# Attention heads three steps later, the first norm's chain in front, and filler transposes on TensorE in a hybrid decoder layer

## The chip, the cores and the metric

One NeuronCore of a Trainium2 chip runs the whole layer. The metric is device time in microseconds (us), the median of several executions. A profiled execution gives the trace that is read below. Engine names are those of the profile: PE is TensorE (PEld its weight loads), DVE is VectorE, ACT is ScalarE, POOL is GpSimd, SP is SyncE, whose queue issues nearly all DMAs.

## The reference

One decoder layer on 256 tokens of width 1024, in float32. A conditioning vector gives shifts, scales and gates by one matrix product. The normed and modulated input goes through one projection whose columns are attention q, k, v (8 heads of 64) and mLSTM q, k (with a causal convolution), v, output gate and gate inputs (4 heads of 128). With 256 tokens the attention is one causal block.

```python
mod = jax.nn.silu(c) @ w_ada[l] + b_ada[l]
sh1, sc1, g1, sh2, sc2, g2 = jnp.split(mod, 6, axis=-1)
h = modulate(x, norm1_g[l], sh1, sc1)          # rms_norm(x) * (1 + sc1) + sh1
proj = h @ w_in[l]
q_a, k_a, v_a, qk_m, v_m, o_m, gates = jnp.split(proj, offs, axis=-1)
attn = merge_heads(moba_attention(rope(q_a), rope(k_a), v_a))
attn = head_rms_norm(attn, attn_out_g[l], ATT_HEADS)
qk_m = jax.nn.silu(causal_conv(qk_m, conv_w[l], conv_b[l]))
hm = mlstm_chunkwise(q_m, k_m * MLSTM_HEAD_DIM ** -0.5, v_m, i_pre, f_pre)
hm = head_rms_norm(hm, mlstm_out_g[l], MLSTM_HEADS) * jax.nn.sigmoid(o_m)
x = x + g1 * (jnp.concatenate([attn, hm], axis=-1) @ w_out[l])
h2 = modulate(x, norm2_g[l], sh2, sc2)
x = x + g2 * hier_moe(h2, ...)                 # 32 experts, top 2 of 8 in the top group
return rms_norm(x, norm_f_g)
```

## The kernel before

All weights stream from HBM through a ring of 23 SBUF slots of 1 MB. A list (`order`) fixes the sequence of the transfers: `wa` (conditioning), `wi` (input projection), `wo` (output projection), then `we`, 192 MB of expert weights. SP issues them in that sequence, each as soon as the slot that it takes has been given back. Everything up to the router, about the first third of the time, is called the front here; after it the experts run quad by quad (`ffn1`, `ffn2`).

Projections keep float32 accuracy by a split of each weight row block: ACT copies it rounded (`whb`, line 210), POOL subtracts (`wlb`, line 211), and PE multiplies three times (lines 494, 495, 497). Four split buffers turn round; `split_to` and `ahead` say how far the splits run ahead of their use.

The start. `xt` (the input) arrives; 16 transposes (`tp`) turn it; four copies take it out of PSUM into `xT`, two on DVE and two on ACT (`x_evac`). Meanwhile ACT squares `xt`, and `norm1_scale` (five small DVE operations, lines 340 to 344) makes the reciprocal norm `r1`; `norm1_rows` spreads it along rows (`rd` on ACT, `rp` on PE, `R1` on ACT). `ada_half(j, h)` computes 256 columns of the conditioning (16 matmuls `adap`, line 404, and a DVE copy into `rowb`), `ada_half_cols` turns them into columns (line 414) and adds the bias (`modc`, line 416). `mod_scale` multiplies `xT` by scale and norm on DVE (line 462), `mod_shift` makes `hh` and the shifted `xT` on ACT (lines 466, 467), `mod_lo` the low part `hl` (line 470). The first projection matmuls `pk` need `hh`, `whb` and `wlb`. Rope angles (two Sin activations on ACT, lines 280 and 284) come right behind. Up to the sixth weight block of k, q and v, the instructions are pinned: their order on the engine is the order of the code.

Behind that, a list scheduler sets the order on each engine, with the order of the code as priority. `pc` are the matmuls of the convolved mLSTM q and k, `po` those of the output gate, `pvm` those of mLSTM v, `op` those of the output projection; each runs over eight k blocks. `side` is a list of attention steps, and `step()` takes one: `attn_s(h)` (scores `s_ps`, DVE row maxima, ACT exponentials `ex`), `attn_t(h)` (transposes `pt_ps`, copied to `ptT`) and `attn_pv(h)` (`pv_ps`). With head 7, `attn_fin` norms all heads on DVE (lines 681 to 689) into `cat`, whose transposes are `ct`. `ml_e(h)` makes the decay matrices (`mb_ps` on PE, `ee` on ACT, a select on POOL), `em_cols` the column `em` (`pmc`, DVE line 711, ACT line 712), `ml_s` and `ml_pv` the mLSTM products (`ms_ps`, `mpv`). `late_rows` computes three more blocks of the conditioning (16 matmuls `adap`, line 431, copied by ACT line 435), `late_cols` their columns (`modp`).

Of the kernel before, what the change touches and what calls it, by code (L numbers as in the profile page):

```python
# [28 lines left out]
MLS = (0, 1, 2, 3)  # L29
CT = (3, 5)  # L30
PIN = 24
MACS = (1, 1, 0, 0)
SLOTS = 23
KEEP = 9
# [3 lines left out]
def tile_hybrid_layer(  # L38
# [11 lines left out]
    nc = tc.nc  # L50
    V, A, G, T = nc.vector, nc.scalar, nc.gpsimd, nc.tensor
# [8 lines left out]
    def pacc(name):  # L60
        return ps.tile([128, 512], F32, name=name, tag="acc", bufs=4)
# [4 lines left out]
    def pA(name):  # L66
        return ps.tile([128, 512], F32, name=name, tag="A", bufs=1)
# [47 lines left out]
    nissued = [0]  # L115
# [3 lines left out]
    def behind(i):  # L119
        ins = i.ins  # L120
        prev = next((x for x in reversed(nc.cur_bb.bb.instructions)
                     if x is not ins and x.engine == ins.engine and x.name not in floating), None)
        tc.add_manual_dep(ins, prev.name, mybir.DependencyInfo(mybir.DependencyClass.NoSync,
                                                               mybir.DependencyReason.DATA), reason="order")

# [2 lines left out]
    def P(i):  # L128
        if pinned[0]:
            behind(i)  # L130
# [2 lines left out]
    keep = [KEEP]  # L133

    def issue():
        kind, j, h = order[nissued[0]][:3]
        part = order[nissued[0]][3:]
        if part == (1,):
            nissued[0] += 1
            behind(nc.sync.dma_start(chunks[kind, j, h][:, 1024:2048], srcs[kind][j, :, h * 2048 + 1024:(h + 1) * 2048]))  # L140
            return
        t = ringp.tile([128, 2048], F32, name=f"w{kind}{j}_{h}", tag="w", bufs=SLOTS)
        chunks[kind, j, h] = t
        nissued[0] += 1
        live[0] += 1
        if part == (0,):
            behind(nc.sync.dma_start(t[:, 0:1024], srcs[kind][j, :, h * 2048:h * 2048 + 1024]))
        elif nissued[0] <= len(order) - 4:
            i = nc.sync.dma_start(t, srcs[kind][j, :, h * 2048:(h + 1) * 2048])
            if nissued[0] < PIN:  # L150
                behind(i)
        elif nissued[0] == len(order):
            for c, n in LAST:
                for key in order[-4:]:
                    src = srcs["e"][key[1], :, h * 2048:(h + 1) * 2048].rearrange("p (f n) -> p f n", f=4)
                    behind(nc.sync.dma_start(chunks[key][:, 4 * c:4 * (c + n)].rearrange("p (f n) -> p f n", f=4),  # L156
                                             src[:, :, c:c + n]))
# [5 lines left out]
    def free(n=1, hold=1):  # L163
        live[0] -= n
        keep[0] += hold
        fill()

    def fill():
        while nissued[0] < len(order) and (live[0] + keep[0] < SLOTS or order[nissued[0]][3:] == (1,)):
            issue()  # L170
# [6 lines left out]

    nc.sync.dma_start(xt, x.rearrange("(t p) d -> p t d", p=128))
    rowb = big("rowb", [128, 2048])
    nc.scalar.dma_start(rowb[:, 1536:1996], colp[:, 96:556])  # L180
    convw = rowb[:, 1536:1568].rearrange("p (i c) -> p i c", i=4)
    wgate = rowb[:, 1568:1632].rearrange("p (k n) -> p k n", k=8)
    wr = rowb[:, 1632:1920].rearrange("p (k n) -> p k n", k=8)
# [10 lines left out]
    def wt(kind, j, k):  # L194
        n = 1024 if kind == "e" else 512
        per = 2048 // n
        return chunks[kind, j, k // per][:, (k % per) * n:(k % per + 1) * n]
# [6 lines left out]
    def split_to(n):  # L204
        while nsplit[0] < min(n, len(subs)):
            i = nsplit[0]
            kind, j, k = subs[i]
            hi, lo = whb[:, i % 4], wlb[:, i % 4]
            src = wt(kind, j, k)
            P(A.activation(hi, src, AF.Copy))  # L210
            G.tensor_tensor(lo, src, hi.bitcast(F32), OP.subtract)  # L211
            parts[kind, j, k] = (hi, lo)
            if k % 4 == 3:
                done()
            nsplit[0] += 1
# [9 lines left out]
    def ahead():  # L225
        split_to(nused[0] + 3)
# [6 lines left out]
    ident = small("ident", [128, 128])  # L233
# [80 lines left out]
    hh = big("hh", [128, 8, S], F32R)  # L314
    hl = big("hl", [128, 8, S], F32R)
    pinned[0] = True
    xps = [pacc(f"tp{kk}") for kk in range(4)]
    for kk in range(4):
        transpose2(xt, kk, xps[kk])

    def x_evac(eng, kk):
        dst, src = xT[:, 2 * kk:2 * kk + 2], xps[kk].rearrange("p (j n) -> p j n", j=2)
        P(V.tensor_copy(dst, src) if eng is V else A.activation(dst, src, AF.Copy))
# [15 lines left out]
    def norm1_scale():  # L339
        P(V.tensor_scalar(v1, ss1, 1.0 / D, EPS, op0=OP.mult, op1=OP.add))  # L340
        P(V.reciprocal(r1, q1))
        P(V.tensor_tensor(q1, r1, r1, OP.mult))
        P(V.scalar_tensor_tensor(q1, q1, -0.5, v1, op0=OP.mult, op1=OP.mult))
        P(V.scalar_tensor_tensor(r1, q1, 1.5, r1, op0=OP.add, op1=OP.mult))
# [66 lines left out]
    def ada_half_cols(half):  # L411
        j, h, p, r = half
        for b in range(2):
            P(T.matmul(p[:, 256 + b:257 + b], r[:, b * 128:(b + 1) * 128], gsel[:, 0:1], start=True, stop=True))
        c0 = 4 * j + 2 * h
        P(V.tensor_tensor(modc[:, c0:c0 + 2], p[:, 256:258], bada[:, c0:c0 + 2], OP.add))
# [6 lines left out]
    def late_cols():  # L423
        j, r = late.pop(0)
        ada_cols(j, r, psm, gsel)
# [34 lines left out]
    def mod_scale(m):  # L460
        for k in range(2 * m, 2 * m + 2):
            P(V.scalar_tensor_tensor(xT[:, k], xT[:, k], a1[:, k:k + 1], R1, op0=OP.mult, op1=OP.mult))

    def mod_shift(m):
        for k in range(2 * m, 2 * m + 2):
            P(A.activation(hh[:, k], xT[:, k], AF.Identity, bias=modc[:, k:k + 1]))
            P(A.activation(xT[:, k], xT[:, k], AF.Identity, bias=modc[:, k:k + 1]))
# [3 lines left out]

    G.memset(wg32, 0.0)
    x_evac(V, 0)
    x_evac(V, 1)
    x_evac(A, 2)
    x_evac(A, 3)
    half = ada_half(2, 0)
    norm1_scale()
    norm1_rows()
    ada_half_cols(half)  # L480
    mod_a1(0)
    half = ada_half(0, 0)
    ahead()
    mod_scale(0)
    ada_half_cols(half)
    mod_shift(0)


    def ip(p, j, k):
        wh, wl = take("i", j, k)  # L490
        ahead()
        ts = [(t, slice(t * 128, (t + 1) * 128)) for t in range(2)]
        for t, tt in ts:
            P(T.matmul(p[t], hh[:, k, tt], wh, start=k == 0, stop=False))  # L494
            P(T.matmul(p[t], hh[:, k, tt], wl, start=False, stop=False))  # L495
        for t, tt in ts:
            P(T.matmul(p[t], hl[:, k, tt], wh, start=False, stop=k == 7))  # L497
# [135 lines left out]
    def attn_s(h):  # L633
        p = psm("s_ps")
        b, o = h // 2, 64 * (h % 2)
        for t in range(2):
            T.matmul(p[:, t * 128:t * 128 + 128 * (t + 1)], qT[o:o + 64, b, t * 128:(t + 1) * 128],  # L637
                     kT[o:o + 64, b, 0:128 * (t + 1)], start=True, stop=True)
        dg = p.rearrange("p (b n) -> p b n", b=4)[:, 0:3:2, :]
        V.tensor_tensor(dg, dg, cmask[:, None, :].to_broadcast([128, 2, 128]), OP.add)  # L640
        V.tensor_reduce(mx[:, h, 0:1], p[:, 0:128], AX.X, OP.max)
        V.tensor_reduce(mx[:, h, 1:2], p[:, 128:384], AX.X, OP.max)
        V.tensor_scalar(mx[:, h], mx[:, h], -0.125, None, op0=OP.mult)
        e = u2("ex", [128, 384])
        for t in range(2):
            A.activation(e[:, t * 128:t * 128 + 128 * (t + 1)], p[:, t * 128:t * 128 + 128 * (t + 1)], AF.Exp,
                         scale=0.125, bias=mx[:, h, t:t + 1], accum_out=rs[:, h, t:t + 1])
        att[h] = e
# [58 lines left out]
    def em_cols():  # L707
        pmc = pY("pmc")
        for t in range(2):
            T.transpose(pmc[:, t * 4:t * 4 + 4], mr[:, t * 128:(t + 1) * 128], ident[0:4, 0:4])  # L710
        behind(V.tensor_tensor(em, nF, pmc[:, 0:8].rearrange("p (t n) -> p t n", t=2), OP.subtract))
        A.activation(em, em, AF.Exp)
# [20 lines left out]


    g1b = wk.tile([128, D], F32, name="g1b", tag="g1b")
    side = [lambda: attn_s(0), lambda: attn_s(1)]

    def t_then_s(h):
        attn_t(h)
# [14 lines left out]
    def step():  # L754
        if side:
            side.pop(0)()
# [3 lines left out]
    for k in range(8):  # L760
        cvk(pc, 3, k)
        step()
        mac(MACS[0])
    conv(pc, 3)
# [4 lines left out]
    for k in range(8):  # L769
        cvk(pc, 4, k)  # L770
        step()
        mac(MACS[1])
    conv(pc, 4)
    while side:
        step()
    free()
    cols()
    row_bcast(modc[:, 20:24], g1b[:, 512:1024])
    A.activation(cv[:, 0:4], cv[:, 0:4], AF.Silu)
    A.activation(cv[:, 4:8], cv[:, 4:8], AF.Silu)  # L780

    po = [pacc("po0"), pacc("po1")]
    em_cols()
    for k in range(8):
        ip(po, 6, k)
        if k % 2 == 0:
            ml_e(k // 2)
        if k in (1, 4, 7):
            late_rows(7 + k // 3)
        if k in (2, 5):  # L790
            late_cols()
    free()
    for t in range(2):
        A.activation(cat[:, t, 512:1024], po[t], AF.Tanh, scale=0.5)
# [574 lines left out]
```

## Time and profile before

| what | value |
|---|---|
| runs shown | 649.70, 648.49, 649.06 us, median 649.06 |
| profiled execution, its own time | 649.01 us |
| its span in the trace | 647.4 us |
| PE busy | 563.3 us, 87% of the span |
| DVE, ACT, POOL busy | 170.2, 144.0, 103.7 us |
| bytes moved by DMA | 248.31 MB, mean 384 GB/s |
| mean granted TensorE clock | 0.973 of full speed |

The span runs from the first to the last instruction; the own time holds 1.61 us more, which lie around it. Busy time of PE is modelled and says that PE had work, not that it ran at its peak. The share of a whole span is a mean over stages with different limits, so the stages are read one by one below.

### The profile page before, as it was taken

To read this page: it belongs to the slowest core of one execution; us is meant where nothing else is said; L and a number is where in the kernel's file an instruction comes from. 1 tells how busy PE (TensorE), PEld (TensorE's weight loads), DVE (VectorE), ACT (ScalarE), POOL (GpSimd) and SP (SyncE) were. 2 spreads that over 40 slices of the span, in tenths; PEclk is the share of its full clock that TensorE was granted. 3 is DMA by queue.
4 is the path that set the end of the run, shared out by engine and by line. 5 is a ranking of instruction groups with operands and counts; after the bars stand their busy time and mean duration, and the time that the engine had idled before them with its cause. 6 is when DMAs were issued, how large, how long until landed. Compare 5 with 4: busy or idle time off the path is not lost.

```text
span 647.4 us, 7994 instructions
## 1 busy us (share of the span) xinstructions
PE 563.3 (87%) x3178; PEld 275.3 (43%) x3178; DVE 170.2 (26%) x448; ACT 144.0 (22%) x306; POOL 103.7 (16%) x98
## 2 busy tenths in 40 slices
PE   4899989999997999998889869877988798889874
PEld 3576878875685444352123214211421332233122
DVE  1533979852745030220002002000100110100013
ACT  5453567854443110000000000000000000001013
POOL 2566746672630000000000000000000000000000
PEclk9799999998996999999989999998999999999998
DMA  8999963699696899999999999999999999999994
GB/s 339 423 425 425 415 264 103 245 353 377 220 403 251 330 427 427 427 425 425 428 428 427 425 427 427 429 426 426 426 428 427 426 425 428 425 426 426 428 383 148
DMA packets 41640, 248.31 MB, mean 384 GB/s; under 512 B 4352, under 2 KB 10624, under 8 KB 12928
## 3 DMA queue, kind: packets, MB, share of 16 engines
q1 hardware_dynamic: 41024, 247.00, 92.5%
q10 hardware_dynamic: 576, 0.76, 0.3%
q8 instruction: 26, 0.43, 0.2%
q14 instruction: 14, 0.11, 0.1%
HBM read 246.70 MB, written 1.05 MB: 383 GB/s over the span
## 4 chain that ended last, share of the span: by engine, by line
DMA 50%; PE 36%; DVE 8%; ACT 2%; SPq 2%; issue 1%; DVEq 0%; ACTq 0%
DMA we<-in_wexp_dram 49%; PE f L1124 4%; PE f1a L1103 3%; PE f1b L1103 3%; PE xg_ps L1024 2%; SPq L156 2%; PE adap L404 1%; PE acc L1136 1%; DVE rowb L366 1%; PE xg_ps L1038 1%; DMA xt<-in_x_dram 1%; DVE ropd L563 1%; PE s_ps L637 1%; PE pk L494 1%; PE pk L495 1%
## 5 line engine op out<-in xcount | busy, mean ns | idle before, releaser
L1103 PE MATMUL f1a<-we,xgt 128*32 128x512 f32 x512 | 134.1, 605 | 30.2 <-DMA we<-in_wexp_dram 30.2
L1103 PE MATMUL f1b<-we,xgt 128*32 128x512 f32 x512 | 133.0, 594 | 0.0
L1124 PE MATMUL f<-we,htb 128*32 128x512 f32 (+2 forms) x576 | 82.8, 572 | 17.3 <-DMA we<-in_wexp_dram 17.3
L211 POOL TENSOR_TENSOR wlb<-wi,whb 128x512 fp32r<-128x512 f32 x56 | 74.6, 1349 | 56.4 <-ACT whb L210 48.8
L1103 PEld LDWEIGHTS f1a<-we,xgt 128*32 128x32 f32 x512 | 23.9, 109 | 105.0 <-DMA we<-in_wexp_dram 81.0
L1103 PEld LDWEIGHTS f1b<-we,xgt 128*32 128x32 f32 x512 | 32.7, 109 | 72.6 <-issue 69.8
L1109 ACT ACTIVATE sab<-f1a 128x256 f32<-128x256 f32 x8 | 3.1, 384 | 247.0 <-PE f1a L1103 247.0
L1110 DVE TENSOR_TENSOR acb<-sab,f1a 128x256 f32<-128x256 f32 x8 | 3.4, 422 | 202.6 <-ACT sab L1109 202.6
L1124 PEld LDWEIGHTS f<-we,htb 128*32 128x32 f32 x576 | 21.2, 113 | 64.9 <-DMA we<-in_wexp_dram 31.6
L210 ACT ACTIVATE whb<-wi 128x512 fp32r<-128x512 f32 x56 | 34.5, 632 | 26.8 <-PE pv L497 7.6
L1130 DVE TENSOR_TENSOR ysb<-f,g2b 128x512 f32<-128x512 f32 (+2 forms) x18 | 11.4, 632 | 93.1 <-PE f L1124 93.1
L1024 PEld LDWEIGHTS xg_ps<-gsb,xt 128*128 128x128 f32 x224 | 26.7, 191 | 13.3 <-issue 7.9
L1029 ACT ACTIVATE xgt<-xg_ps,modc,a 128x128 f32<-128x128 f32 x28 | 10.5, 457 | 93.2 <-PE xg_ps L1024 93.2
L1024 PE MATMUL xg_ps<-gsb,xt 128*128 128x128 f32 x224 | 28.6, 279 | 1.9 <-ACT xgt L1029 1.9
L1136 PE MATMUL acc<-ysb,pwb 128*128 128x512 f32 x56 | 27.3, 613 | 2.5 <-DVE ysb L1130 2.3
L211 POOL TENSOR_TENSOR wlb<-wo,whb 128x512 fp32r<-128x512 f32 x16 | 21.0, 1317 | 23.7 <-ACT whb L210 23.2
L366 DVE SCALAR_TENSOR_TENSOR rowb<-wa,cs,rowb 128x512 f32<-128x512 f32 x21 | 23.9, 1139 | 0.3
L506 PE MATMUL pc<-hl,whb 128*128 128x256 f32 x64 | 18.4, 289 | 0.0
L505 PE MATMUL pc<-hh,whb 128*128 128x256 f32 x64 | 18.2, 286 | 0.0
L1136 PEld LDWEIGHTS acc<-ysb,pwb 128*128 128x128 f32 x56 | 9.6, 189 | 19.2 <-issue 8.9
L507 PE MATMUL pc<-hh,wlb 128*128 128x256 f32 x64 | 17.7, 289 | 0.0
L1012 DVE TENSOR_TENSOR gsb<-iot,posm 128x128 f32<-128x128 f32 x16 | 4.4, 289 | 35.7 <-PE xg_ps L1024 32.1
(371 smaller groups left out, 691.5 us busy)
## 6 DMA issues: line engine op xcount, KB each, us to landing
we<-in_wexp_dram SPq DMA_DIRECT2D x188, 1024.0 KB, 19.6
wa<-in_wada_dram SPq DMA_DIRECT2D x24, 1024.0 KB, 13.6
wi<-in_win_dram SPq DMA_DIRECT2D x8, 1024.0 KB, 18.4
wi<-in_win_dram SPq DMA_DIRECT2D x12, 512.0 KB, 14.0
wo<-in_wout_dram SPq DMA_DIRECT2D x4, 1024.0 KB, 7.2
we<-in_wexp_dram SPq DMA_DIRECT2D x4, 512.0 KB, 16.8
we<-in_wexp_dram SPq DMA_DIRECT2D x8, 256.0 KB, 6.3
xt<-in_x_dram SPq DMA_DIRECT2D x1, 1024.0 KB, 5.7
```

The lines of the kernel that those rows point to most:

```text
L156: behind(nc.sync.dma_start(chunks[key][:, 4 * c:4 * (c + n)].rearrange("p (f n) -> p f n", f=4), src[:, :, c:c + n]))
L210: P(A.activation(hi, src, AF.Copy))
L211: G.tensor_tensor(lo, src, hi.bitcast(F32), OP.subtract)
L366: i = V.scalar_tensor_tensor(r, w, cs[:, k:k + 1], r, op0=OP.mult, op1=OP.add)
L505: T.matmul(o, wh[:, cc], hh[:, k], start=k == 0 and c % 2 == 0, stop=False)
L506: T.matmul(o, wh[:, cc], hl[:, k], start=False, stop=False)
L507: T.matmul(o, wl[:, cc], hh[:, k], start=False, stop=k == 7 and c % 2 == 1)
L1024: T.matmul(p[:, (k % 4) * 128:(k % 4 + 1) * 128], xn[:, t, k * 128:(k + 1) * 128], gsb[:, q % 2, t], start=t == 0, stop=t == 1)
L1103: T.matmul(hid[h][CAP * i:CAP * (i + 1), :], xgb[q % 2][:, k, i * CAP:(i + 1) * CAP], w[:, h * 512:(h + 1) * 512], start=k == 0, stop=k == 7)
L1124: m = T.matmul(py[CAP * i:CAP * (i + 1), 0:n], htb[:, f // 2, o:o + CAP], chunks["e", 3 * (4 * q + i) + 2, dh][:, w0:w0 + n], start=f == 0 ...
L1130: V.tensor_tensor(ysb[q % 2][:, c0:c0 + n], py[:, 0:n], g2b[:, c0:c0 + n], OP.mult)
L1136: T.matmul(acc[b], pwb[:, q % 2, t * 128:(t + 1) * 128], ysb[q % 2][:, h * 512:(h + 1) * 512], start=q == 0, stop=q == NQ - 1 - h)
```

## The change

It has three parts. First, the side list begins with three empty steps, and the steps left over are taken in the output gate's loop (`po`) and behind it, not behind the second convolution; `em_cols` moves behind them. Second, in the start `norm1_scale` stands right behind the first copy, the two copies on ACT stand behind `mod_shift(0)`, only two weight blocks are split ahead and not three, and the transfer of the small tables (`rowb`, 230 KB) leaves ACT's queue and stands sixth among SP's weight transfers. Third, TensorE transposes the identity into an unused PSUM tile: 28 times before `xt` arrives, and 4, 4 and 8 times in the first chain; nothing reads the result.

```diff
+SHIFT = 3
+WARM = 28
...
     def issue():
+        if nissued[0] == 5:
+            behind(nc.sync.dma_start(rowb[:, 1536:1996], colp[:, 96:556]))
         kind, j, h = order[nissued[0]][:3]
...
     rowb = big("rowb", [128, 2048])
-    nc.scalar.dma_start(rowb[:, 1536:1996], colp[:, 96:556])
...
     pinned[0] = True
+    wp = pA("warm")
+
+    def fillers(n):
+        for _ in range(n):
+            P(T.transpose(wp[:, 0:128], ident, ident))
+
+    fillers(WARM)
     xps = [pacc(f"tp{kk}") for kk in range(4)]
...
     x_evac(V, 0)
+    norm1_scale()
     x_evac(V, 1)
-    x_evac(A, 2)
-    x_evac(A, 3)
     half = ada_half(2, 0)
-    norm1_scale()
+    fillers(4)
     norm1_rows()
     ada_half_cols(half)
     mod_a1(0)
     half = ada_half(0, 0)
-    ahead()
+    fillers(4)
     mod_scale(0)
+    split_to(2)
     ada_half_cols(half)
+    fillers(8)
     mod_shift(0)
+    x_evac(A, 2)
+    x_evac(A, 3)
...
-    side = [lambda: attn_s(0), lambda: attn_s(1)]
+    side = [lambda: None] * SHIFT + [lambda: attn_s(0), lambda: attn_s(1)]
...
     conv(pc, 4)
-    while side:
-        step()
-    free()
+    step()
     cols()
...
     po = [pacc("po0"), pacc("po1")]
-    em_cols()
     for k in range(8):
         ip(po, 6, k)
+        step()
         if k % 2 == 0:
             ml_e(k // 2)
...
+    while side:
+        step()
+    free()
+    em_cols()
     free()
```

On ACT at the start, the order before is this, from the squares of `xt` to the first Sin (`hl` is only where the squares are thrown):

```order
L330 ACTIVATE hl,ss_169<-xt 128x1024 x2
L337 ACTIVATE q_177<-ss_169,epsb 128x2
L323 ACTIVATE xT<-tp_151 128x512
L323 ACTIVATE xT<-tp_152 128x512
L349 ACTIVATE rd<-ident,r_176 128x128 x2
L351 ACTIVATE R_179<-rp 128x256
L210 ACTIVATE whb<-wi_0_82 128x512 x2
L210 ACTIVATE whb<-wi_0_84 128x512
L466 ACTIVATE hh<-xT,modc 128x256
```

And of the change, up to the third weight split:

```order
L349 ACTIVATE q_206<-ss_198,epsb 128x2
L361 ACTIVATE rd<-ident,r_205 128x128 x2
L363 ACTIVATE R_208<-rp 128x256
L215 ACTIVATE whb<-wi_0_81 128x512 x2
L478 ACTIVATE hh<-xT,modc 128x256
L479 ACTIVATE xT<-xT,modc 128x256
L335 ACTIVATE xT<-tp_180 128x512
L335 ACTIVATE xT<-tp_181 128x512
L285 ACT_TABLE_LOAD
L285 ACTIVATE rt<-rt 128x64
L289 ACTIVATE rt<-rt 128x64
L215 ACTIVATE whb<-wi_0_83 128x512 x2
```

The two copies have left the norm's way, and the third split (`wi_0_84` before, `wi_0_83` now, the first block of q) has moved from ahead of `hh` to behind the two Sin activations.

On PE, around the last attention head (`pv_ps`, head 7) and the end of the mLSTM v matmuls (`pvm`), the order before is:

```order
L494 MATMUL pvm_1377<-whb,hh 128x512
L666 MATMUL pv_ps<-v_sb,ptT 128x64
L667 MATMUL pv_ps<-v_sb,ptT 128x64
L668 MATMUL pv_ps<-v_sb,ptT 128x64
L718 MATMUL mb_ps<-misc 128x256
L431 MATMUL adap<-wa_0_556,cs 32x512 x4
L431 MATMUL adap<-wa_1_605,cs 32x512 x4
L495 MATMUL pvm_1377<-wlb,hh 128x512
```

And of the change, where the three rows of `pv_ps` are again head 7:

```order
L512 MATMUL pvm_1421<-whb,hl 128x512
L512 MATMUL pvm_1422<-whb,hl 128x512
L669 MATMUL pt_ps<-ident,ex 128x128 x3
L443 MATMUL adap<-wa_0_601,cs 32x512 x4
L443 MATMUL adap<-wa_1_650,cs 32x512 x4
L681 MATMUL pv_ps<-v_sb,ptT 128x64
L682 MATMUL pv_ps<-v_sb,ptT 128x64
L683 MATMUL pv_ps<-v_sb,ptT 128x64
L733 MATMUL mb_ps<-misc 128x256
L406 MATMUL modp<-gsel,rowb 128x1 x4
L725 MATMUL pmc<-ident,misc 128x4 x2
L733 MATMUL mb_ps<-misc 128x256
```

Before, 21 `pvm` matmuls, one block `adap` and one `mb_ps` follow head 7; now they all stand ahead of it, and behind it come three `mb_ps`, two blocks `adap`, three groups `modp` and the products up to `ct`.

## Rows read from the trace of the kernel before

**Rows 1.** Stretches of the span: busy time by engine, PEclk, DMA share, GB/s.

```profile
204.00:212.00 8.00, 7.48 (x48) 4.43 (x48) 2.80 (x14) 0.91 (x2) 0.00 (x0) 0.68 0.02 7
220.00:640.00 420.00, 364.32 (x1920) 125.28 (x1912) 44.11 (x114) 26.00 (x67) 0.00 (x0) 0.99 1.00 419
```

**Rows 2.** SP's queue in time: start, length, issues from the list `order`.

```profile
212.28 2.06 SPq L149 DMA_DIRECT2D we<-in_wexp_dram  x4
```

**Rows 3.** The stretch of the front from the first projection matmul on.

```profile
20.40:137.00 116.60, 113.05 (x731) 91.30 (x735) 74.61 (x162) 71.18 (x142) 72.55 (x55) 0.98 0.82 327
```

**Rows 4.** Start in time: start, length, instruction, idle time before it and releaser.

```profile
7.24 3.65 PE L309 MATMUL tp<-ident,xt 128*128 128x128 f32 x16 [7.24 <-DMA xt<-in_x_dram]
9.41 0.30 ACT L337 ACTIVATE q<-ss,epsb 128x2 f32<-128x2 f32 x1
10.81 1.19 PE L404 MATMUL adap<-wa,cs 128*32 128x256 f32 x16
12.08 0.42 DVE L408 COPY rowb<-adap 128x256 f32<-128x256 f32 x1 [2.18 <-PE adap L404]
13.33 0.69 ACT L349 ACTIVATE rd<-ident,r 128x128 f32<-128x128 f32 x2 [1.81 <-DVE r L344]
15.06 1.93 PE L404 MATMUL adap<-wa,cs 128*32 128x256 f32 x16
17.40 2.37 DVE L462 SCALAR_TENSOR_TENSOR xT<-xT,a,R 128x256 f32<-128x256 f32 x2
19.88 0.51 ACT L466 ACTIVATE hh<-xT,modc 128x256 fp32r<-128x256 f32 x1 [3.33 <-DVE modc L416]
```

**Rows 5.** Line 462 over the span: ns shortest, median, longest.

```profile
L462 DVE SCALAR_TENSOR_TENSOR xT<-xT,a,R x8: 478/485/1479, 17.4 to 54.9; 128x256 f32<-128x256 f32 x8
```

**Rows 6.** The first split and those behind the Sin activations, in time.

```profile
15.59 3.90 POOL L211 TENSOR_TENSOR wlb<-wi,whb 128x512 fp32r<-128x512 f32 x3 [11.48 <-ACT whb L210]
...
25.21 1.66 ACT L210 ACTIVATE whb<-wi 128x512 fp32r<-128x512 f32 x3
...
25.91 6.28 POOL L211 TENSOR_TENSOR wlb<-wi,whb 128x512 fp32r<-128x512 f32 x5 [6.41 <-ACT whb L210]
...
26.72 0.39 PE L495 MATMUL pq<-wlb,hh 128*128 128x512 f32 x1
```

**Rows 7.** Three stretches, columns as in Rows 1, for the granted clock.

```profile
14.50:24.60 10.10, 7.67 (x35) 5.36 (x34) 5.91 (x19) 5.41 (x10) 3.90 (x3) 0.50 1.02 426
147.00:151.00 4.00, 3.17 (x30) 1.55 (x22) 0.00 (x0) 3.94 (x10) 1.76 (x3) 1.00 0.96 367
151.00:154.60 3.60, 3.60 (x18) 0.67 (x17) 0.16 (x1) 0.12 (x1) 0.54 (x2) 0.53 0.94 355
```

**Rows 8.** PE in time, from the first head's transposes to `ct`.

```profile
91.43 0.33 PE L654 MATMUL pt_ps<-ident,ex 128*128 128x128 f32 x1 [0.62 <-ACT ex L646]
...
135.97 0.39 PE L668 MATMUL pv_ps<-v_sb,ptT 128*128 128x64 f32 x2
...
146.55 1.92 PE L431 MATMUL adap<-wa,cs 128*32 128x512 f32 x16
...
155.28 1.05 PE L394 MATMUL modp<-gsel,rowb 128*128 128x1 f32 x8
...
159.59 1.04 PE L309 MATMUL ct<-ident,cat 128*128 128x128 f32 x8
```

**Rows 9.** The chain that ended last: two of the `pvm` matmuls.

```profile
130.47 0.46 PE pvm L497 x2
```

**Rows 10.** The attention norm's chain and what ran beside it, in time.

```profile
140.53 2.68 POOL L211 TENSOR_TENSOR wlb<-wo,whb 128x512 fp32r<-128x512 f32 x2
140.58 1.27 DVE L301 TENSOR_TENSOR ar_q<-ar_y 128x16 f32<-128x16 f32 x1
...
143.28 0.17 DVE L301 TENSOR_TENSOR ar_q<-ar_y 128x16 f32<-128x16 f32 x1
...
146.57 0.21 ACT L712 ACTIVATE em<-em 128x8 f32<-128x8 f32 x1 [1.26 <-DVE em L711]
```

More of the change, by code (lines that the diff above doesn't have):

```diff
@@ L122, in behind @@
                      if x is not ins and x.engine == ins.engine and x.name not in floating), None)
+        if prev is None:
+            return
         tc.add_manual_dep(ins, prev.name, mybir.DependencyInfo(mybir.DependencyClass.NoSync,
```

## The prediction

> **What bounds the kernel now.** I first read the stretches of the span. From 220 to 640 us the DMA engines are at 1.00 and move 419 GB/s [rows 1]: that is the expert stream, and nothing in it is changed. So the end is fixed by the moment at which the stream becomes continuous. Before it lies a hole: from 204 to 212 us the DMA share is 0.02 [rows 1]. SP's queue in time says why it ends: SP resumes at 212.28 [rows 2], when the first expert matmuls give slots of the ring back; until then all 23 are full. A front that ends earlier frees these slots earlier, and the end follows one to one as long as the hole lasts (8 us); a front that ends later moves the end one to one too. Then the front itself: from the first projection matmul at 20.4 to 137 us PE is busy 113.05 of 116.6 us [rows 3], so it is PE's work, in a fixed amount, that sets the pace, and a shift of the first matmul is passed on. Two places are left where PE is not fully used: the start, up to 20.4, and the tail of attention, from head 7 to `ct` at 159.59 [rows 8]. The change works on both. The profiled execution took 649.01 us, 0.05 under the median of the runs shown; I make the sum against 649.0. Differences under 0.2%, 1.3 us, are about what a measurement of this kernel can't tell from no change.
>
> **The start: what comes earlier.** In the start in time, ACT ends `q` at 9.71, but `rd` begins only at 13.33 [rows 4]: the five small DVE operations stand behind the `rowb` copy, which waits 2.18 us for PE and ends at 12.50. They take 13.33 − 12.50 = 0.83 us. Put behind the first copy they end at 9.71 + 0.83 = 10.54, and `rd` (0.69) ends at 11.23. PE then must be free for `rp`. The 16 transposes took 3.65 us, 0.228 each, against 1.04 / 8 = 0.13 each at `ct` [rows 4, 8], so at the start PE runs at its lower level though the profile's column doesn't say so. With 28 fillers ahead I expect the upper level: transposes 7.24 + 2.1 = 9.3, `adap` 1.19 to 10.5, four fillers (0.5) to 11.0: free in time. At the lower level it is 12.00 as before plus 0.5 to 0.9, so 1.3 to 1.7 us later. From the end of `rd` to the second `adap` block it was 15.06 − 14.02 = 1.04 us; so this block starts at 12.3, takes 1.19 at the upper level (1.93 at the lower, as now), and its copy and what surrounds it took 17.40 − 16.99 = 0.41. Line 462 starts at 13.9 and not at 17.40.
>
> **A price that depends on POOL.** The two operations of line 462 took 2.37 us, though the line takes 0.485 each when alone; its longest is 1.479 [rows 4, 5], and POOL ran `wlb` from 15.59 to 19.49 beside it [rows 6]. Now POOL has two and not three operations there, in about the same place, so the pair takes 0.97 to 2.37; I take 1.7. With 0.11 us to ACT as now, `hh` starts at 13.9 + 1.7 + 0.1 = 15.7 and not at 19.88: 4.2 us earlier (1.1 with PE at the lower level and POOL in the way, 4.9 at best). The Trainium skill, "SBUF — State Buffer", section "SBUF: two separate sides", says that a DVE operation with two SBUF inputs and a GpSimd operation that reads SBUF exclude each other for a whole instruction; 1479 against 485 ns agrees. By that rule as it stands the pair would take 2.37 again, `hh` come at 16.4 and the sum be 0.7 higher, 645.6, inside the forecast's own range.
>
> **What is given back.** The third split now stands behind the Sin activations. These follow `hh` through a chain on DVE and ACT that does not change, and before, the splits behind them began 25.21 − 19.88 = 5.33 us (ACT) and 6.03 us (POOL) after `hh`; one POOL split takes 6.28 / 5 = 1.26 [rows 6]. So `wlb` of the first q block is there 7.3 us after `hh`; before, its matmul ran 26.72 − 19.88 = 6.84 after [rows 6]. That loses 0.4. It also makes PE wait ahead of that matmul. Between 14.5 and 24.6 the granted clock was 0.50 [rows 7], after PE had stood from 12.00 on until `rd` was there [rows 4]; the fillers and the shorter waits may keep it up, which makes the k matmuls faster but only lengthens the wait for q. If the clock then falls as it did from 151 to 154.6 (0.53 for 3.6 us [rows 7]), it costs 3.6 × 0.47 = 1.7. Between nothing and 1.7 I take 0.8. The two copies moved on ACT (1.2 us) fit where ACT waits for DVE's rope chain. The 28 fillers take at most 28 × 0.228 = 6.4 us and lie before `xt` lands, the others in PE's waits; at worst they delay the transposes by 0.9, which the norm's chain doesn't see until `rp`. Moving 230 KB off ACT's queue may bring `xt` forward by up to 230 KB / 426 GB/s [rows 7] = 0.5; I take 0.2. Start: 4.2 + 0.2 − 0.4 − 0.8 = **3.2 us** (0.3 to 4.9).
>
> **The tail.** Before, head 7's `pv_ps` ends at 135.97 + 0.39 = 136.36, and behind it PE still has 21 `pvm` matmuls at 0.23 [rows 9], one block `adap` of 1.92 [rows 8] and a pair of `mb_ps` (0.5, an estimate from two `pvm`). All these now lie ahead: 136.36 + 4.8 + 1.9 + 0.5 = 143.6. Head 7's `ptT` copy stands behind more work on ACT (0.5, an estimate), and the wait of 0.62 at 91.43 [rows 8] is filled, since weight matmuls stand in that place: 143.5. From there to `ct` was 159.59 − 146.55 = 13.0 us of PE order, and two pairs of `mb_ps` and a group `modp` (1.05 [rows 8]) come to it, 2.2 together. `ct` is due at 143.5 + 15.2 = 158.7: **0.9 us** earlier, beside the start's shift. This holds if nothing in the norm's chain is waited for. That chain runs from `pv_ps` on DVE to `em` on ACT at 146.57 [rows 10], 10.2 us after head 7. In it small DVE operations took 1.27 and not 0.17 us while POOL ran `wlb<-wo` [rows 10]; three of these make about 3 us. In the new order POOL has all four `wlb<-wo` ahead of head 7's end, so the chain is 7.2 us, and with 1.9 (an estimate) from `em` to the `rowb` copy of the third block, `modp` is free 9.1 us after head 7; PE arrives there after about 9.0. If POOL is still in the way, PE waits 3 us.
>
> **The clock in the tail.** It fell to 0.53 at 151, though PE had been busy for 3.17 of the 4.0 us before in small matmuls [rows 7]. I leave one such stretch in the sum; without it `ct` comes 1.7 earlier, with a second 1.7 later. So the tail lies between 0.9 − 1.7 = −0.8 and 0.9 + 1.7 = 2.6. The Trainium skill, "TensorE: Matmul & The Clock Gate", Part 1, section "What's actually happening", says that activity releases the throttle and an idle stretch sets it again; the row shows a fall with hardly an idle stretch. By the page's sentence the tail would keep the upper level and the sum would be 1.7 lower, 643.2, the lower end of the forecast's own range.
>
> The rest is free of charge: SP's order changes by one small transfer, `free()`'s later place moves nothing in it, and the heads' DVE and ACT work goes under `po`, where PE is the one that is busy. Sum: 649.0 − 3.2 − 0.9 = **644.9 us**.
>
> **Rivals.** *More*: `hh` at its earliest, no fall of the clock: start 4.6, tail 2.6, 641.8. For it, [rows 5] at 485 ns; against it, the clock fell on lesser occasions. *Little*: PE is still at its lower level up to `rp`, so that the start gives 1.1, and the tail nothing: 647.9. For it, that PE stood at 0.50 for ten us [rows 7]. *Slower*: attention's end lies bare. With the heads late, POOL still holds DVE and the chain takes 10.2: `em` at 143.5 + 10.2 = 153.7, `modp` at 155.6, PE stands, and from there to `ct`, 4.3 us now (155.28 to 159.59 [rows 8]), it runs at the lower level, 8.6: `ct` at 164.2, 4.6 late, less 3.2 from the start: 650.4. It decides once `ct`, counted without the start's shift, comes later than 159.6 + 3.2 = 162.8. *Nothing*: the shift is absorbed, since the ring is not full at 204 or the hole is set by the transfers themselves: 649.0; against it, the DMA share of 0.02.
>
> **Chances.** Forecast case 0.58, its own range 643.2 to 646.8; more 0.17; little 0.14; slower 0.08; nothing 0.03. The range from 641.8 to 648.3 takes in the first three but for their ends and leaves out the rest, some 0.2 in all. Under 647.7 lie the forecast, more, and half of little: 0.82; within 1.3 us the other half and nothing: 0.11; slower 0.07.
>
> **What the changed profile would show.** Right: `hh` at about 15.7; transposes at 0.13 us; the first q matmul 7 us behind `hh` with PE waiting for the split; `ct` at 155.5 (158.7 less the start's 3.2); SP resuming near 208, and the hole half as long. Wrong: the clock at 0.50 from the first k matmul far past 25 us; PE waiting for `modp` or `ct` behind the norm's chain; a hole of unchanged length while `ct` is early. The prediction fails most easily on the clock, whose level I can only take over from the rows.

## The result and the profile after

The change makes the kernel slower: 654.28 us median of 13 executions (649.10 to 659.33) against 648.49 before, ratio 1.0074 with a 95% interval of 1.0049 to 1.0098. The forecast was 644.9. The executions spread over 10 us and the mean granted clock goes roughly with them: 649.10 us came with 0.973, 659.33 with 0.961. The profiled execution is the one of 659.33, over 1.5% above the fastest; it counts as a slow one and is left out of the ratio, so a second profile of the change (e4_again, 655.70) stands beside it wherever a number matters.

The start in time, profile of the change:

```profile
1.62 5.13 PE L326 MATMUL warm<-ident 128*128 128x128 f32 x28 [1.62 <-POOL ident L240]
6.85 1.97 PE L314 MATMUL tp<-ident,xt 128*128 128x128 f32 x16
...
10.29 0.69 ACT L361 ACTIVATE rd<-ident,r 128x128 f32<-128x128 f32 x2 [0.88 <-DVE r L356]
...
13.51 1.89 DVE L474 SCALAR_TENSOR_TENSOR xT<-xT,a,R 128x256 f32<-128x256 f32 x2
...
15.50 0.51 ACT L478 ACTIVATE hh<-xT,modc 128x256 fp32r<-128x256 f32 x1 [1.36 <-DVE modc L428]
...
22.86 0.80 PE L510 MATMUL pq<-wlb,hh 128*128 128x512 f32 x1 [0.86 <-POOL wlb L216]
```

Beside [rows 4, 6]: the transposes take 0.123 us each and not 0.228, `hh` begins at 15.50 and not at 19.88, the first q matmul that needs `wlb` at 22.86 and not at 26.72, so 3.9 us of the start's lead are alive there. At the first matmul `pc` 2.3 of them are left (65.07 against 67.38): from 24 to 28 us the clock of the change is at 0.76. In e4 it is at 1.00 there, and `pc` begins at 63.55. The tail in time, from the products of head 7 to `ct`:

```profile
147.82 0.39 PE L683 MATMUL pv_ps<-v_sb,ptT 128*128 128x64 f32 x2
148.14 0.69 PE L733 MATMUL mb_ps<-misc 4*128 4x256 f32 x2
148.76 1.05 PE L406 MATMUL modp<-gsel,rowb 128*128 128x1 f32 x8
...
151.32 2.79 PE L443 MATMUL adap<-wa,cs 128*32 128x512 f32 x16
154.04 1.22 PE L733 MATMUL mb_ps<-misc 4*128 4x256 f32 x2
155.19 1.87 PE L406 MATMUL modp<-gsel,rowb 128*128 128x1 f32 x8
156.98 3.64 PE L443 MATMUL adap<-wa,cs 128*32 128x512 f32 x16
...
166.43 1.04 PE L314 MATMUL ct<-ident,cat 128*128 128x128 f32 x8
```

Beside [rows 8]: head 7 ends 11.8 us later (148.21 against 136.36) and `ct` 6.8 us later (166.43 against 159.59). A block `adap` of 16 matmuls is 1.92 us at the upper level; here two of them take 2.79 and 3.64. SP's queue, beside [rows 2]:

```profile
222.99 2.06 SPq L155 DMA_DIRECT2D we<-in_wexp_dram  x4
```

The stretches, with the columns of [rows 1]: the hole, the stream, and two low stretches of the clock (the column behind the five engines; 1.00 is the upper level, 0.50 the lower).

```profile
216.00:222.00 6.00, 6.00 (x39) 3.02 (x42) 0.83 (x3) 0.92 (x2) 0.00 (x0) 0.62 0.02 4
230.00:640.00 410.00, 355.77 (x1822) 118.37 (x1814) 41.12 (x107) 22.92 (x54) 0.00 (x0) 0.99 1.01 426
135.30:138.80 3.50, 3.50 (x19) 3.40 (x18) 0.00 (x0) 0.49 (x1) 0.00 (x0) 0.53 0.92 344
152.50:162.20 9.70, 9.70 (x40) 4.34 (x32) 2.97 (x12) 2.76 (x7) 1.08 (x4) 0.50 0.96 371
```

The hole is still there, SP resumes 10.7 us later (222.99 against 212.28), and the execution is 10.3 us longer (659.33 against 649.01): the end follows the front nearly one to one, as the prediction had it. So the question is how 3.9 us of lead at the first q matmul become 6.8 us of delay at `ct`.

### The profile page after: what moved, and what is told of

Its sections match the earlier page's. It is cut to its first block, busy times and chain, and to the rows that moved or that the text cites. A ratio compares the mean times of both kernels' runs of the same rounds, so it can differ in the third digit from the quotient of the medians.

```text
span 656.8 us, 8084 instructions
## 1 busy us (share of the span) xinstructions
PE 576.7 (88%) x3222; PEld 284.7 (43%) x3222; DVE 168.9 (26%) x448; ACT 144.9 (22%) x306; POOL 103.5 (16%) x98
## 3 DMA queue, kind: packets, MB, share of 16 engines
HBM read 246.70 MB, written 1.05 MB: 377 GB/s over the span
## 4 chain that ended last, share of the span: by engine, by line
DMA 49%; PE 36%; DVE 8%; ACT 2%; SPq 2%; issue 1%; POOL 0%; DVEq 0%; ACTq 0%
DMA we<-in_wexp_dram 49%; PE f1a L1120 3%; PE f L1141 3%; PE f1b L1120 3%; DVE rowb L378 2%; PE xg_ps L1041 2%; SPq L162 2%; PE acc L1153 1%; PE adap L443 1%; PE adap L416 1%; PE s_ps L652 1%; PE xg_ps L1055 1%; PE modp L406 1%; DVE ropd L578 1%; DMA xt<-in_x_dram 1%
## 5 line engine op out<-in xcount | busy, mean ns | idle before, releaser
L1120 PE MATMUL f1a<-we,xgt 128*32 128x512 f32 x512 | 132.5, 608 | 28.6 <-DMA we<-in_wexp_dram 28.6
L1120 PE MATMUL f1b<-we,xgt 128*32 128x512 f32 x512 | 131.3, 597 | 0.0
L1141 PE MATMUL f<-we,htb 128*32 128x512 f32 (+2 forms) x576 | 84.6, 584 | 17.1 <-DMA we<-in_wexp_dram 16.9
L216 POOL TENSOR_TENSOR wlb<-wi,whb 128x512 fp32r<-128x512 f32 x56 | 76.0, 1371 | 51.7 <-ACT whb L215 51.1
L1147 DVE TENSOR_TENSOR ysb<-f,g2b 128x512 f32<-128x512 f32 (+2 forms) x18 | 11.4, 632 | 92.0 <-PE f L1141 92.0
L378 DVE SCALAR_TENSOR_TENSOR rowb<-wa,cs,rowb 128x512 f32<-128x512 f32 x21 | 25.6, 1219 | 0.3
L1048 DVE TENSOR_SCALAR xgt<-xg_ps,a,modc 128x128 f32<-128x128 f32 x28 | 9.6, 404 | 20.2 <-PE xg_ps L1041 20.2
```

The lines of the kernel that those rows point to most:

```text
L378: i = V.scalar_tensor_tensor(r, w, cs[:, k:k + 1], r, op0=OP.mult, op1=OP.add)
L1120: T.matmul(hid[h][CAP * i:CAP * (i + 1), :], xgb[q % 2][:, k, i * CAP:(i + 1) * CAP], w[:, h * 512:(h + 1) * 512], start=k == 0, stop=k == 7)
L1141: m = T.matmul(py[CAP * i:CAP * (i + 1), 0:n], htb[:, f // 2, o:o + CAP], chunks["e", 3 * (4 * q + i) + 2, dh][:, w0:w0 + n], start=f == 0 ...
L1147: V.tensor_tensor(ysb[q % 2][:, c0:c0 + n], py[:, 0:n], g2b[:, c0:c0 + n], OP.mult)
```

## Experiments

Every edit is against the change unless it says otherwise; every ratio is to the kernel before on the same chip, where its median was 648.8 to 649.7 us. The experiments ran on four chips, so two of them are compared by these ratios, not by their medians.

**Which part costs.** e1 keeps the heads' part and puts the start of before back; e2 keeps the start and puts the heads back; e3 leaves the fillers out; e4 is the change again.

```diff
 # e1_heads
+    nc.scalar.dma_start(rowb[:, 1536:1996], colp[:, 96:556])
...
-    fillers(WARM)
...
     x_evac(V, 0)
-    norm1_scale()
     x_evac(V, 1)
+    x_evac(A, 2)
+    x_evac(A, 3)
     half = ada_half(2, 0)
-    fillers(4)
+    norm1_scale()
...
 # e2_start
-    side = [lambda: None] * SHIFT + [lambda: attn_s(0), lambda: attn_s(1)]
+    side = [lambda: attn_s(0), lambda: attn_s(1)]
     conv(pc, 4)
-    step()
+    while side:
+        step()
+    free()
...
 # e3_nofill
-        for _ in range(n):
+        for _ in range(0 * n):
```

> Heads three steps later, the start as before. Theory A (the heads' part costs, the start still gives some 2 to 4 us): 653 to 659 us against 648.5 before, with head 7's last product at about 150 us and ct near 168. Theory B (the start moves the clock's falls, the heads are harmless): 647 to 649.5. Theory C (the two parts cost only together): 648 to 650.

658.51 us, ratio 1.0116 (1.0069 to 1.0162).

> The new start alone, fillers included, heads where they were before. Theory A: 644.5 to 646.5 us, the q matmuls 3.9 us earlier, as in the profile of the change, and most of that left at ct (156 to 158 against 159.6). Theory B: 651 to 656, with granted clock below 0.97. Theory C: 647 to 650.

646.05 us, ratio 0.9942 (0.9915 to 0.9970): faster than before.

> The change with all 44 fillers left out. Theory A: the start loses its high clock and some 1 to 3 us of its lead, the tail stays as in the change: 654 to 658 us. Theory B, if the fillers are what moves the clock's falls: 648 to 650 with a clock of 0.97 and more.

657.54 us, ratio 1.0096 (1.0062 to 1.0130).

> The change once more, for a second profile beside the others on the same chip: 649 to 659 us with a median near 654 under every theory. Theory A: ct is late by 3 us or more in this profile too, also where its mean clock is high. Theory B: ct is late only by what the clock takes, so at a clock of 0.97 it comes earlier than 159.6.

658.14 us, ratio 1.0106 (1.0055 to 1.0157). Theory A holds in all four: the start gains 3.7 us, and the heads' part costs 8.8 (e1) to 12 us (e4 less e2). What the 44 fillers bring by themselves is not shown: without them (e3) the time is that of e4. In e3's profile the 16 transposes take 3.65 us, as before, `hh` begins at 16.61 and the q matmul that needs `wlb` at 23.96; with them, in the profiles of the new start, these come at 15.11 to 16.59 and 22.48 to 23.93. In e4's profile `ct` is at 163.48; in e2's it is at 157.1, though the first q matmul is at the same place in both (22.5 and 22.6). `em_cols` and `free()` are not to blame: with SHIFT = 0 and all else of the heads' part in place, the order of instructions on every engine is that of e2.

TensorE waits in a place where it did not before. The third `modp` from `ones` (block 6 of the conditioning) in the profile of before, of e2 and of e4, each with its idle time:

```profile
131.71 0.95 PE L394 MATMUL modp<-ones,rowb 128*128 128x1 f32 x8
```

```profile
129.30 0.95 PE L406 MATMUL modp<-ones,rowb 128*128 128x1 f32 x8
```

```profile
130.76 1.05 PE L406 MATMUL modp<-ones,rowb 128*128 128x1 f32 x8 [1.69 <-DVE rowb L378]
```

DVE makes the sums for it, 128x512 at a time, between the row maxima of the heads. The last of them in e2 and in e4:

```profile
123.38 4.32 DVE L378 SCALAR_TENSOR_TENSOR rowb<-wa,cs,rowb 128x512 f32<-128x512 f32 x3
```

```profile
127.17 3.54 DVE L378 SCALAR_TENSOR_TENSOR rowb<-wa,cs,rowb 128x512 f32<-128x512 f32 x2
```

In e2 they end at 127.70; in e4 row maxima of the later heads stand in between, and they end at 130.71. Behind the wait the clock falls, in e4's stretches of 2 us:

```profile
130.00:132.00 2.00, 1.24 (x10) 1.20 (x11) 1.02 (x3) 0.00 (x0) 1.83 (x2) 1.00 0.36 57
132.00:134.00 2.00, 2.00 (x10) 1.83 (x9) 0.02 (x1) 0.00 (x0) 0.00 (x0) 0.54 0.78 274
134.00:136.00 2.00, 2.00 (x13) 2.00 (x12) 0.00 (x0) 0.49 (x1) 0.00 (x0) 0.61 1.04 418
```

The loss there is 1.69 + 2 × 0.46 + 2 × 0.39 = 3.4 us.

**Size of the shift.**

```diff
 # e5_shift1, e6_shift2
-SHIFT = 3
+SHIFT = 1      (2 in e6)
```

> The change with heads one step later and not three. Theory W (what costs is each wait of TensorE that is followed by a stretch at the low clock, and the low clock in the tail; the wait for the conditioning rows and the blocks behind head 7 make them): 646 to 649 us, since the tail's order is nearly that of before, with at most one wait of over 1 us ahead of it. Theory O (the time follows the amount of work that is put behind head 7, about evenly with each step, 646 without a shift and 654 to 658 with three): 649 to 651.

652.22 us (647.76 to 662.05), ratio 1.0040 (1.0012 to 1.0068): above both theories. No wait for DVE's sums shows in its profile, but TensorE waits 1.33 us for ACT's `ee` in the tail, and from 80 to 92 us the clock is at 0.68, 0.50 and 0.54 in stretches of 4 us, which takes 5.1 us (4.00 × (0.32 + 0.50 + 0.46)); e4 loses 1.7 there, e2 nothing.

> The change with heads two steps later. TensorE's order has head 7's product ahead of one block of the conditioning and 12 of the mLSTM v matmuls, so the tail is covered. Theory W: 646 to 650 us. Theory O: 651 to 654.

646.50 us, ratio 0.9952 (0.9938 to 0.9966), as W has it; its profile is of an execution of 652.85 us and does not show what the median did. One step is slower than two, so the time does not follow the amount of work put behind the heads (theory O). That it follows the waits is not shown by these two; for three steps the next runs look at it.

**The wait in the middle.** e7 moves block 6 of the conditioning behind the mLSTM v matmuls; e9 fills the wait.

```diff
 # e7_cols_late
     conv(pc, 4)
     step()
-    cols()
-    row_bcast(modc[:, 20:24], g1b[:, 512:1024])
...
+    cols()
+    row_bcast(modc[:, 20:24], g1b[:, 512:1024])
     free(3, 0)
 # e9_mid_fill, in ada_cols
         p = pf("modp")
+        if one is None and j == 6:
+            for _ in range(12):
+                behind(T.transpose(p[:, 128:256], ident, ident))
```

> The change, with the columns of the conditioning block 6 and their spreading over the rows (modp from ones, gbp) moved behind the mLSTM v matmuls, so that TensorE does not wait 1.69 us for DVE's sums there. Theory W: the low clock behind that wait goes too, 3 to 4 us less than the change: 651 to 654, ct near 160 in the profile. Theory O: the work is only moved, 654 to 658.

Here the columns are read when their row buffer already holds another block, so values and the choice of experts are others, and the 3505.09 us say nothing of the change. Only the front, whose work is the same in kind and amount, is read: `ct` at 160.7 against 163.5 in e4. Since 2.6 us of matmuls (`modp` and `gbp`) went behind `ct`, that alone does not show that the low clock went too.

> The change, with 12 transposes of the identity ahead of the third modp from ones; nothing reads their result; they take 1.6 us at the upper level, and 6 matmuls of mLSTM v slip in front of it too. TensorE's order from the heads to ct is otherwise that of the change. Theory W: the wait of 1.69 us ahead of it and the low clock behind it (3 to 4 us of it at half speed) go; ct about 3 us earlier less the fillers' 1.6: 652 to 656. Theory O (order alone): the time rises by the fillers' 1.6 us, 656 to 660.

648.76 us (646.55 to 659.49), ratio 0.9997 (0.9969 to 1.0025): by the two ratios 0.8%, 5.0 us, under the change, more than either theory gave. The same stretch of its profile, where TensorE goes from the 12 transposes (from 131.29 on) to the `modp` (132.60) without idle time:

```profile
130.00:132.00 2.00, 2.00 (x19) 1.92 (x18) 0.98 (x2) 1.12 (x2) 2.00 (x3) 1.00 0.32 53
132.00:134.00 2.00, 2.00 (x21) 2.00 (x19) 0.16 (x1) 0.00 (x0) 1.18 (x1) 1.00 0.72 258
134.00:136.00 2.00, 2.00 (x14) 1.60 (x14) 0.00 (x0) 0.76 (x2) 0.00 (x0) 1.00 1.03 422
```

The wait and the fall behind it are both gone. This profiled execution took 654.39 us and still has the clock at 0.50 to 0.70 from 144 to 160 us, so the tail is a second loss of its own.

**The tail.** e8 fills it behind each group `modp`, e10 fills both, e13 and e14 only make the late `modp` matmuls 64 columns wide, e13 with the order of the change on TensorE, VectorE and GpSimd up to the experts. On ScalarE three `ee` stand ahead of `em` in e13 and behind it in the change, and some products of the experts come in another order; e14 has the order of e9 on every engine, and e15 that of e11.

```diff
 # e8_tail_fill (e10_mid_tail: with the lines of e9 too), in ada_cols
+        if one is not None and j < 10:
+            for _ in range(8):
+                behind(T.transpose(p[:, 128:256], ident, ident))
 # e13_wide (e14_mid_wide: with the lines of e9 too), in ada_cols
+        w = 64 if one is not None and j < 10 else 1
         for b in range(4):
-            T.matmul(p[:, b:b + 1], r[:, b * 128:(b + 1) * 128], (one or ones)[:, 0:1], start=True, stop=True)
+            T.matmul(p[:, b * w:b * w + w], r[:, b * 128:(b + 1) * 128],
+                     (ones if one is None else one)[:, 0:1].to_broadcast([128, w]), start=True, stop=True)
```

> The change, with 8 transposes of the identity behind each of the three groups modp of the tail; nothing reads their result; they take 1.0 us a group at the upper clock level. Theory W, if it is the small matmuls of the tail that keep the clock low: the granted clock from 148 to 160 us rises from about 0.55 to over 0.8, and the time is 653 to 657. Theory O or a clock that follows something else: the clock stays, and the time is 3 to 4 us above the change, 658 to 661.

652.07 us, ratio 1.0060 (1.0035 to 1.0085): by the ratios 0.9 us under the change, with overlapping intervals, so no faster that can be told, though 3.1 us more work is in it. Its profile has no low clock between 140 and 200 us.

> The change with both fillers, the 12 of the middle and the 8 behind each group modp of the tail. Theory W: no low clock from 128 to 175 us, ct near 160 to 161 in spite of 4.7 us of added matmuls: 648 to 651. Theory O: 656 to 661.

653.94 us, ratio 1.0067 (1.0044 to 1.0090): between the two theories. The clock of its profile is 0.50 to 0.77 from 144 to 160 us although no idle time of TensorE over 0.4 us stands ahead of it. So transposes behind the narrow matmuls do not hold the clock reliably, and a wait is not the only thing that ends in a low clock.

> The change, with the matmuls of the three groups modp in the tail 64 columns wide and not one; the extra columns repeat the first, and the order of all engines is the same. Theory N (narrow matmuls of the tail set off its low clock): the clock from 148 to 160 us rises to over 0.85 and the time falls by 3 to 5: 651 to 654. Theory G (the low clock there comes from the waits and from where the stretch before it ended): clock near 0.55 and 654 to 658, as the change.

650.76 us (646.89 to 652.53), ratio 1.0028 (1.0013 to 1.0043): by the ratios 0.46%, 3.0 us, under the change, as theory N has it, though the two intervals only just stay apart (up to 1.0043 here, from 1.0049 there), and no execution above 652.6. The profile is of an execution of 646.89 us, the least of 13 (the others took 649.89 to 652.53), so it shows a tail without a fall and not what each execution did. It runs within 0.1 us of e4's up to 148 us (head 7 ends at 145.26 in e4 and at 145.29 here). Then e4:

```profile
144.87 0.39 PE L683 MATMUL pv_ps<-v_sb,ptT 128*128 128x64 f32 x2
...
147.75 0.69 PE L733 MATMUL mb_ps<-misc 4*128 4x256 f32 x2 [0.67 <-ACT ee L736]
148.37 2.84 PE L443 MATMUL adap<-wa,cs 128*32 128x512 f32 x16
...
152.29 1.87 PE L406 MATMUL modp<-gsel,rowb 128*128 128x1 f32 x8
154.09 3.64 PE L443 MATMUL adap<-wa,cs 128*32 128x512 f32 x16
...
163.48 1.04 PE L314 MATMUL ct<-ident,cat 128*128 128x128 f32 x8
```

and e13:

```profile
144.90 0.39 PE L685 MATMUL pv_ps<-v_sb,ptT 128*128 128x64 f32 x2
...
147.77 0.69 PE L735 MATMUL mb_ps<-misc 4*128 4x256 f32 x2 [0.61 <-ACT ee L738]
148.39 1.92 PE L445 MATMUL adap<-wa,cs 128*32 128x512 f32 x16
...
151.03 1.11 PE L407 MATMUL modp<-gsel,rowb 128*128 128x64 f32 x8
152.07 1.92 PE L445 MATMUL adap<-wa,cs 128*32 128x512 f32 x16
...
159.01 1.04 PE L314 MATMUL ct<-ident,cat 128*128 128x128 f32 x8
```

The clock there, in e4 and in e13:

```profile
148.00:152.00 4.00, 4.00 (x20) 1.03 (x19) 3.43 (x17) 2.10 (x5) 1.09 (x4) 0.65 1.01 426
152.00:156.00 4.00, 4.00 (x21) 2.37 (x24) 0.86 (x4) 1.35 (x4) 0.54 (x2) 0.50 0.93 338
156.00:160.00 4.00, 4.00 (x23) 2.17 (x12) 0.56 (x1) 0.60 (x1) 0.00 (x0) 0.57 0.98 391
```

```profile
148.00:152.00 4.00, 3.91 (x28) 1.74 (x27) 3.43 (x16) 3.11 (x8) 1.07 (x4) 1.00 1.00 424
152.00:156.00 4.00, 4.00 (x32) 2.36 (x31) 1.70 (x6) 1.07 (x3) 0.91 (x2) 1.00 0.94 330
156.00:160.00 4.00, 4.00 (x34) 3.87 (x33) 1.85 (x5) 1.08 (x3) 0.00 (x0) 1.00 0.99 399
```

With the wait of 0.6 us in both, the same order on TensorE, and only the width of eight matmuls a group changed on it, `ct` comes 4.5 us earlier: every `adap` takes 1.92 us.

> The 12 transposes of the middle (648.8 us by themselves, in two groups of executions near 648 and 654) with the 64 columns in the tail. Theory N: the upper group goes, 645 to 648. Theory G: 647 to 651, with both groups still there.

649.67 us (646.44 to 652.60), ratio 1.0011 (0.9989 to 1.0034): no better than e9, and still in two groups, 646.4 to 647.9 and 649.6 to 652.6, as theory G has it; but e9's executions at 654 to 659 are gone.

**A version that beats both.** e11 is e2 with 24 transposes where TensorE waits for the choice of experts; e12 the same with SHIFT = 2; e15 is e11 with the wide matmuls.

```diff
     logits(1, 1)
+    wr2 = psm("rfill")
+    for _ in range(24):
+        behind(T.transpose(wr2[:, 0:128], ident, ident))
     xn = xt
```

> The new start alone, with 24 transposes of the identity where TensorE waits 3.24 us for the choice of experts; nothing reads their result. In the profile of the new start alone the clock was 0.50 from 200 to 206 us behind this wait, in 5.27 us of matmuls. Theory W: the clock stays up there, 2 to 3 us less than the new start alone: 643 to 644.5. Theory O, or a clock that falls anyway: 646, as the new start alone.

643.07 us (640.75 to 647.33), ratio 0.9909 (0.9880 to 0.9938). In the profile of e2 the stretch behind that wait is

```profile
199.00 0.64 PE L1005 MATMUL pp<-mk,us 128*128 128x32 f32 x2 [3.24 <-DVE mk L1002]
...
202.08 3.75 PE L1053 MATMUL xg_ps<-gsb,xt 128*128 128x128 f32 x16 [0.73 <-DVE gsb L1027]
```

and in e11

```profile
194.48 2.82 PE L962 MATMUL rfill<-ident 128*128 128x128 f32 x24
197.89 0.41 PE L1008 MATMUL pp<-mk,us 128*128 128x32 f32 x2 [0.59 <-DVE mk L1005]
...
199.93 2.02 PE L1056 MATMUL xg_ps<-gsb,xt 128*128 128x128 f32 x16 [0.73 <-DVE gsb L1030]
```

The gather `xg_ps` takes 2.02 and not 3.75 us, and the first expert matmul comes 4.00 us behind the start of `pp` and not 6.76: 2.8 us. By the ratios e11 is 0.33%, 2.1 us, under e2, with overlapping intervals.

> The same 24 transposes, with heads two steps later and the new start. Theory W: 643.5 to 645, against 646.5 without them. Theory O: 646.5.

644.12 us, ratio 0.9919 (0.9886 to 0.9952): by the ratios again 2.1 us under the same kernel without the transposes (e6), as theory W has it.

> The new start alone with the 24 transposes at the choice of experts (643.1 us) and the 64 columns in the tail. Theory N: the low stretch near 148 to 152 us goes, 641 to 642.5. Theory G: 642.5 to 644.

644.01 us, ratio 0.9907 (0.9876 to 0.9937): at the upper end of theory G; without the change's tail the wide matmuls bring nothing that can be measured. Its profile has no fall in the tail but one from 174 to 182 us, where e11's has none. From head 7 to `ct` the profiles lose to the low clock (length of a stretch times what its clock lacks to 1.00, added up) 5.1 us in e4 and nothing in e13, 6.8 in e9 and 1.7 in e14, 1.7 in e11 and nothing in e15: less with 64 columns in all three pairs, with one profile of each kernel.

## Why the prediction was wrong

**The bound: right.** The hole, SP's resumption and the end moved together.

**The start: right.** 3.2 us were forecast, e2 measures 3.7 (649.72 to 646.05). `hh` was forecast at 15.7 and came at 15.50; the pair of line 462 (now 474) was put at 1.7 and took 1.89; the transposes ran at 0.123 us; the q matmul's `wlb` came 22.86 − 15.50 = 7.4 us behind `hh`, 7.3 were forecast. The 0.8 for a fall of the clock is a mean that neither profile has: at the first `pc` the lead is 2.3 us in the change, with a fall, and 3.8 in e4, without. That the fillers raise the level of the transposes is shown (e3), that the time needs them is not.

**The end of head 7: wrong, and the first step that failed.** The prediction counted the matmuls that stand ahead of head 7 in the new order and took TensorE as busy throughout: "the wait of 0.62 at 91.43 is filled, since weight matmuls stand in that place", 143.5 without the start's shift. And it put the heads' other work at nothing: "the heads' DVE and ACT work goes under `po`, where PE is the one that is busy". The matmuls were counted rightly. But the later heads also push DVE's conditioning sums back, and TensorE now waits 1.69 us for the last of them. A second new wait, of 1.22 to 1.24 us, stands at the first `modp` from `ones` near 84 to 88 us in the change, e1 and e13; in e4 a stretch at 0.62 from 80 to 84 us takes its place and costs 1.7 with its end at 85 us. In e4 head 7 ends at 145.26; with the lead at the first matmul `pc` (63.55 against 67.38 before) that is 149.1 in the prediction's count, 5.6 later than forecast. 3.4 of it are the wait in the middle with its low clock: in e9, without both, head 7 ends 2.6 us earlier than in e4 although 1.5 us of transposes were added ahead of it. 1.7 are the stretch at 0.62, which no run with later heads is rid of together with the wait; 0.5 is not assigned. In the change head 7 is 7.0 late by the same count (148.21 + 2.31 = 150.5): 3.4 for the middle, 2.9 for the second wait and the low clock behind it (0.65 from 88 to 92 us), 0.7 not assigned.

**The tail's clock: the wrong size.** "I leave one such stretch in the sum; without it `ct` comes 1.7 earlier, with a second 1.7 later." From head 7 to `ct` 15.2 us were forecast; it took 18.2 in the change (148.21 to 166.43) and in e4, and 13.7 in e13, where the clock stayed up. So the low clock costs 4.5 us there, not the 1.7 of the sum, and `ct` comes 3.0 later than forecast for it. Head 7's move leaves two blocks `adap` and three groups `modp` between it and `ct`; with these groups one column wide the stretch behind them ran at 0.50 to 0.65, with 64 columns at 1.00. That their width sets off the fall is made likely by the three pairs of profiles and not shown beyond them: e14 falls with 64 columns, and e8 does not with one column and transposes behind.

**Behind `ct`: a fall that was not in the sum.** Behind a wait of 0.59 us the clock in stretches of 2 us is at 0.59, 0.50, 0.50 and 0.70 from 186 to 194 us in the change, and at 0.50 from 184 to 190 us in e4; with its ends the fall costs 3.4 us in each. The profiles of before and e2 have the wait and no fall. Against the forecast the profiles are late by these terms, in us:

| term | e4 | the change |
|---|---|---|
| start: 3.2 forecast, 3.8 and 2.3 left at the first `pc` | −0.6 | 0.9 |
| head 7: the wait in the middle and the clock behind it | 3.4 | 3.4 |
| head 7: the second wait or the low clock there | 1.7 | 2.9 |
| head 7: not assigned | 0.5 | 0.7 |
| tail: 18.2 and not 15.2 | 3.0 | 3.0 |
| behind `ct`: the fall near 190 us | 3.4 | 3.4 |
| sum | 11.4 | 14.3 |
| measured, less 644.9 | 10.8 | 14.4 |

**The norm's chain: right, and the slower rival with its mechanism wrong.** With POOL's `wlb<-wo` out of the way, the small DVE operations take 0.17 to 0.21 us in e4 and `em` is there 7.5 us behind head 7 (7.2 forecast); TensorE waits for no `modp` of the tail. The Trainium skill, "SBUF — State Buffer", section "SBUF: two separate sides", names the lock between VectorE and GpSimd; [rows 10] against these durations agree with it. The rival that ended slower gave 650.4 by a bare norm's chain. Its sign came true, `ct` past 162.8 without the start's shift (163.48 + 3.83 = 167.3 in e4), but by another way.

The Trainium skill, "TensorE: Matmul & The Clock Gate", Part 1, section "What's actually happening", has an idle stretch set the throttle. The middle (1.69 us of waiting, then 0.54) and the wait for the experts (3.24, then 0.50) agree with it; the tail does not agree: e10's clock falls without a wait of over 0.4 us ahead, and e13's stays up behind one of 0.61, with e4's order on TensorE.

**What stays open.** Why executions of one kernel fall into low stretches of different length (649.10 to 659.33 for the change, 647.76 to 662.05 for e5) is not settled; the profiles show that they do, and the falls elsewhere too: behind a wait of 0.59 in the change and in e4, from 174 to 182 us in e15, not in e13, nor in before, which has the wait as well. That e10 is slower than e9 is not explained either, nor that e5, with one step, is slower than e6 with two, beyond the wait and the low stretch named.

## What to carry to other kernels

When work is moved on one engine, follow what it delays on the others: here the moved heads pushed back sums on DVE that TensorE takes later, and a wait of 1.7 us cost 3.4. Count the time of a tail at both clock levels, and try its groups of one-column matmuls wider where that is free: 64 columns took 1.10 us where one took 1.05, and in the profiles compared `ct` came 4.5 us earlier. Where TensorE must wait long for a decision, matmuls that nobody reads are nearly free and can pay: behind 24 transposes the first expert matmul came 2.8 us earlier, and by the ratios the time fell by some 2 us in both kernels that had them, though the intervals overlap.

## What the runs showed of the hardware

In the tail of e4, with groups of eight one-column matmuls, the granted clock is 0.50 to 0.65 from 148 to 160 us, though TensorE is busy by the profile for 4.00 of each 4.00 us; in e13, with 64 columns, it is 1.00 there. It is not without exception: e14 has 64 columns too, and 0.60 from 148 to 152 us, and e8, with one column and 8 transposes behind each group, stays at 1.00 where e10 falls. The clock's column is 1.00 at the start both before and after, while the 16 transposes took 3.65 us before and in e3, and 1.97 after the fillers: there the durations tell the level, not the column.
